# Last MLP: seven block products for the first matrix, the second matrix by pairs of hidden blocks over all tokens, and sums of weight blocks made by adding DMAs during the first MLP

## The chip, the cores and the metric

The kernel runs on one core of one Trainium2 chip. The metric is device time in microseconds (us) from the first to the last instruction of one launch; lower is better. Several executions are timed, and one more is recorded by the hardware profiler. All line numbers below are those of the profile: for the kernel before, "L231" is line 231 of the listing printed further down.

## The reference, cut to what matters

A trunk of two layers works on 1024 tokens with 1024 features. Layer 0 mixes tokens with an mLSTM, layer 1 with latent attention (MLA). After each mixer comes an MLP with a hidden width of 4096.

```python
def sqrelu_mlp(h, w1, w2):
    return jnp.square(jax.nn.relu(h @ w1)) @ w2

# in each layer
h = modulate(rmsnorm(x, g), shift, scale)
x = x + gate * rmsnorm(sqrelu_mlp(h, w1, w2), g2)
```

Everything is float32. `w1` is 1024 x 4096 and `w2` is 4096 x 1024 in each layer. The change concerns `h @ w1` and `... @ w2` of layer 1, for the second half of the tokens.

## The kernel before

**Numbers.** A float32 product is made of three products of a shorter format. Every operand is split into a high part (a cast on ScalarE, L189 for weights) and a low part (a subtraction on VectorE, L190), and `mm3` (L230 to L233) issues three matmuls for each pair of operand tiles: high weight and low weight against high and low data, without the product of the two low parts.

**Stages.** The tokens are worked on in two halves of 512, `hfs[0]` and `hfs[1]`. The four MLP calls run one after another, and the other work is woven between their steps: `mlp(0, hfs[0])` with the background `bg_latent` (the remaining adaLN vectors, the rope tables, the preparation of the latent weights), `mlp(0, hfs[1])` with the layer-1 mixer of the first half, `mlp(1, hfs[0])` with the layer-1 mixer of the second half, and last `mlp(1, hfs[1])`, called here the last MLP. Beside the last MLP runs only `all_out`, the writing of the results: `x_to_rows` transposes the residual stream into rows, `rows_out` normalises the MLP output, adds the residual and stores.

**One MLP.** The hidden width is cut into 32 blocks of 128. `hidden(f)` (L952) makes one block: 8 slices of the 1024 features times 3 matmuls, each 128 x 128 weights against 512 tokens, into one PSUM tile `ps`. ScalarE squares the ReLU of it (L962, L963) and casts it (L471), VectorE makes the low part (L472). `up_rows` (L978) multiplies four hidden blocks by the second matrix for two token blocks at a time, into a PSUM tile `pm` of two banks, and `accumulate` (L971) adds the result to the output in SBUF (VectorE, L198). Steps of both kinds alternate, 24 matmuls of 512 columns each. A step's weights (512 KB) are loaded two steps ahead (`AHEAD`, L944): SyncE's DMA into `raw` (4 buffers), L189 and L190 into `ws` (8 buffers, two per load).

**Order.** Each engine has one queue, in the order that a scheduler gives to the program's instructions. `paced()` (L182) ties an instruction of a background behind the latest weight split, L190. GpSimd has almost nothing to do in this kernel: small DMAs at the start and memsets that claim buffers (L170, L1346). `small(n)` (L144) hands out tiny tiles from 6 buffers.

Of the kernel before, what the change touches and what calls it, by code (L numbers as in the profile page):

```python
# [9 lines left out]
F32 = mybir.dt.float32  # L10
# [72 lines left out]
def kernel(  # L83
# [143 lines left out]

    pe_last = [None]

    def mm3(o, lh, ll, rh, rl, start, stop):  # L230
        nc.tensor.matmul(o, ll, rh, start=start, stop=False)  # L231
        nc.tensor.matmul(o, lh, rl, start=False, stop=False)  # L232
        pe_last[0] = nc.tensor.matmul(o, lh, rh, start=False, stop=stop)  # L233


    nc.scalar.preload_act_table_set("natural_log_exp_and_others")
# [240 lines left out]
    def normed(h, xs_, rstd, A, sh):  # L477

        for k in range(KD):
            with paced():  # L480
                nc.vector.scalar_tensor_tensor(
                    xs_[k], xs_[k], A[:, k : k + 1], rstd, ALU.mult, ALU.mult
                )
                split_mod(h.hi[k], h.lo[k], xs_[k], sh[:, k : k + 1])
            if k % 4 == 3:
                yield 1

# [455 lines left out]
    NF = DFF // P  # L943
    AHEAD = 2  # L944

    def mlp(l, hf, y, sizes, rows=False):


        w1, w2, h = mlp_w1[l], mlp_w2[l], hf.h2
        hids = {}  # L950

        def hidden(f):  # L952
            def hid(w):
# [98 lines left out]
        steps, prev, f0 = [], [], 0  # L1052
        for G in sizes:
            fs = list(range(f0, f0 + G))
            f0, done = f0 + G, 0
            for i in range(G):
# [7 lines left out]
        for n in range(len(steps) + AHEAD):  # L1064
            if n < len(steps):
                ready.append(steps[n][0]())
            if n >= AHEAD:
                yield from steps[n - AHEAD][1](ready.pop(0))

                yield steps[(n - AHEAD + 1) % len(steps)][1].__name__  # L1070


    rope_d = scratch([2, P, S], "rope_d")
# [494 lines left out]

    def x_to_rows(half):

        for k in range(KD):
            a, b = tmc(), tmc()
            nc.sync.dma_start(a, xs_blk(k, half))
            yield
            pt = pc()
            for t in range(4):
                nc.tensor.transpose(pt[:, ts(t, P)], a[:, ts(t, P)], ident)
            nc.scalar.copy(b, pt)
# [19 lines left out]
    def rows_out(hf, y, B):  # L1598

        xt = []  # L1600
        for t in range(4):
            a = k4v()
            r0 = hf.i * H + t * P
            nc.sync.dma_start(a, xr[r0 : r0 + P, :].rearrange("p (a b) -> p a b", b=512))
            xt.append(a)
        yield
        for t in range(4):
            yt, st = y.t[t], small(4)
            for g in range(2):
                junk = ps()  # L1610
                nc.scalar.activation(junk, yt[:, g], AF.Square, accum_out=st[:, g : g + 1])
            ys = [tmc(), tmc()]
            v, r, w = small(1), small(1), small(1)
            with tc.high_priority(PRIO):
                for g in range(2):
                    nc.vector.tensor_mul(ys[g], yt[:, g], B[:, g])
                nc.vector.tensor_scalar(v, st[:, 0:1], st[:, 1:2], 1.0 / D, ALU.add, ALU.mult)
                nc.vector.tensor_scalar_add(v, v, EPS)
                rsqrt_(r, v, w)
            for g in range(2):  # L1620
                nc.vector.scalar_tensor_tensor(ys[g], ys[g], r, xt[t][:, g], ALU.mult, ALU.add)
                r0 = hf.i * H + t * P
                nc.sync.dma_start(out[0, r0 : r0 + P, ts(g, 512)], ys[g])
            yield


# [126 lines left out]
    A1 = gain(2, NG(0, 2), adac(0, SC2))  # L1753
    B1 = gate(3, NG(0, 3), adac(0, G2))

    def post(hf, y, B, src, A, sh):
# [5 lines left out]
        yield 0  # L1762
        hf.h2 = Split()
        yield from normed(hf.h2, y, rstd, A, sh)

# [124 lines left out]
    drain(p1)  # L1890
    two_streams(f0, behind(bg_latent(), 4))
    rope_perm()


    z1 = FH(claim=True)
    ya = [None, None]

    def mixer1(hf, z, attention):
# [12 lines left out]
        for _ in wout(b_w_out[0], hf.o, lambda m, pt: evac(y[m], pt)):  # L1911
            yield 0
        yield 1
        yield from post(hf, y, B2, x_cols, A3, adac(1, SH2))
# [5 lines left out]
    two_streams(mlp(1, hfs[0], u0, [2] * 16, True), mixer1(hfs[1], z1, attention_second))  # L1920
    u1 = FH(claim=True)

    def all_out():
        yield from x_to_rows(0)
# [43 lines left out]
```

## Time and profile before

| what | value |
|---|---|
| median of three runs | 2379.76 us (2376.8 to 2380.19) |
| the profiled execution's own time | 2377.5 us |
| its span, first to last instruction | 2375.5 us |
| granted TensorE clock, mean | 0.997 |
| loads of MLP weights, first and last start | 463.1 us and 2326.6 us |

A row of busy time gives, for each engine (PE is TensorE's matmuls, PEld its weight loads, DVE is VectorE, ACT is ScalarE, POOL is GpSimd, SP is SyncE), microseconds and the number of instructions. A group's row gives line, engine, operation, output and input tiles, count, total busy time, mean duration in ns, then the idle time of its engine just before, with what ended it. A DMA row gives packets, megabytes and the share of 16 DMA engines' time.

### The profile page before, as it was taken

Reading aid. Unit: us, or ns where it says so; the run is one execution under the profiler, and the core shown is the slowest. Engines: PE = TensorE matmul, PEld = TensorE weight load, DVE = VectorE, ACT = ScalarE, POOL = GpSimd, SP = SyncE. Lnnn points to the kernel's source line nnn. Section 1 sums busy time; section 2 is a strip of 40 time slices with the busy share of each in tenths; the row PEclk is TensorE's granted clock in tenths of the full one; section 3 lists DMA queues with packets and bytes.
Section 4 is the critical chain, followed back from the end, with each engine's and each line's share of the span. In section 5 each row is a group of like instructions: output and inputs, shape, how many; then the busy total and the mean of one; then the engine's idle time right before and its main releaser. Section 6 shows DMA issues by size and latency. Waiting matters only on the chain.

```text
span 2375.5 us, 30534 instructions
## 1 busy us (share of the span) xinstructions
PE 2343.4 (99%) x11621; PEld 1946.7 (82%) x11621; DVE 1549.6 (65%) x2435; ACT 1055.6 (44%) x1716; POOL 18.2 (1%) x93
## 2 busy tenths in 40 slices
PE   7999999999999999999999999999999999999998
PEld 5888888788888888888888888888888888888887
DVE  6667866868666667877764967765666486353345
ACT  4355334655333454434443554444444453444333
POOL 1000000000000000000000000000000000000000
PEclk9999999999999999999999999999999999999999
DMA  9452664544664745555543454874434354364431
GB/s 313 149 142 85 186 181 139 168 133 144 186 181 143 250 135 187 160 161 183 182 133 113 147 166 163 249 248 136 148 98 143 114 169 129 102 191 140 144 102 62
DMA packets 377106, 374.48 MB, mean 158 GB/s; under 512 B 24355, under 2 KB 282464, under 8 KB 376960
## 3 DMA queue, kind: packets, MB, share of 16 engines
q1 hardware_dynamic: 376672, 372.44, 50.3%
q8 instruction: 91, 1.49, 0.3%
q14 instruction: 55, 0.45, 0.1%
q0 software_dynamic: 288, 0.10, 0.0%
HBM read 313.24 MB, written 59.24 MB: 157 GB/s over the span
## 4 chain that ended last, share of the span: by engine, by line
PE 89%; DVE 4%; DMA 4%; ACT 1%; issue 1%; SPq 0%; DVEq 0%; ACTq 0%
PE ps L231 16%; PE ps L233 16%; PE ps L232 16%; PE pm L231 9%; PE pm L232 9%; PE pm L233 9%; PE pc L1450 1%; DMA raw<-in_a_w_in_dram 1%; DMA raw<-in_mlp_w_dram 1%; PE pc L231 1%; PE pc L233 1%; PE pc L232 1%; PE pm L1336 1%; DVE wl L190 1%; PE pm L820 1%
## 5 line engine op out<-in xcount | busy, mean ns | idle before, releaser
L190 DVE TENSOR_TENSOR wl<-raw,wh 128x1024 fp32r<-128x1024 f32 (+2 forms) x366 | 438.9, 1202 | 442.7 <-ACT wh L189 435.7
L189 ACT CAST wh<-raw 128x1024 fp32r<-128x1024 f32 (+2 forms) x366 | 377.6, 1035 | 704.3 <-PE ps L231 381.7
L231 PE MATMUL ps<-k,wl 128*128 128x512 f32 x1528 | 605.2, 396 | 2.5 <-ACT k L679 1.4
L233 PE MATMUL ps<-k,wh 128*128 128x512 f32 x1528 | 596.1, 390 | 0.0
L232 PE MATMUL ps<-k,wh 128*128 128x512 f32 x1528 | 595.6, 390 | 0.0
L231 PEld LDWEIGHTS ps<-k,wl 128*128 128x128 f32 x1528 | 287.0, 188 | 65.1 <-issue 2.9
L233 PEld LDWEIGHTS ps<-k,wh 128*128 128x128 f32 x1528 | 286.8, 188 | 61.7 <-issue 0.5
L232 PEld LDWEIGHTS ps<-k,wh 128*128 128x128 f32 x1528 | 287.2, 188 | 58.8 <-issue 1.7
L198 DVE TENSOR_TENSOR k<-k,pm 128x512 f32<-128x512 f32 (+1 forms) x254 | 211.0, 860 | 104.1 <-PE pm L233 103.6
L231 PE MATMUL pm<-hd,wl 128*128 128x512 f32 x512 | 200.9, 392 | 0.5 <-ACT hd L471 0.5
L232 PE MATMUL pm<-hd,wh 128*128 128x512 f32 x512 | 199.3, 390 | 0.2 <-DVE hd L472 0.2
L233 PE MATMUL pm<-hd,wh 128*128 128x512 f32 x512 | 199.2, 389 | 0.0
L231 PE MATMUL pm<-wh,hd 128*128 128x512 f32 x488 | 192.2, 394 | 1.6 <-ACT raw L1342 1.3
L232 PE MATMUL pm<-wl,hd 128*128 128x512 f32 x488 | 190.9, 391 | 0.0
L233 PE MATMUL pm<-wh,hd 128*128 128x512 f32 x488 | 190.2, 390 | 0.0
L359 DVE SCALAR_TENSOR_TENSOR tma<-raw,cond,tma 128x512 f32<-128x512 f32 x168 | 125.6, 748 | 20.4 <-DMA raw<-in_kv_ada_w_dram 14.4
L472 DVE TENSOR_TENSOR hd<-tmp,hd 128x512 fp32r<-128x512 f32 x128 | 88.3, 690 | 54.7 <-ACT hd L471 54.4
L1342 ACT ACTIVATE raw<-pm,sm 128x128 f32<-128x128 f32 (+3 forms) x64 | 47.5, 742 | 150.1 <-DVE sm L1341 121.8
L231 PEld LDWEIGHTS pm<-hd,wl 128*128 128x128 f32 x512 | 96.2, 188 | 20.8 <-ACT hd L471 0.9
L232 PEld LDWEIGHTS pm<-hd,wh 128*128 128x128 f32 x512 | 96.1, 188 | 20.5 <-DVE hd L472 0.5
L233 PEld LDWEIGHTS pm<-hd,wh 128*128 128x128 f32 x512 | 96.1, 188 | 20.2
L231 PEld LDWEIGHTS pm<-wh,hd 128*128 128x128 f32 x488 | 91.6, 188 | 22.3 <-ACT raw L1342 3.5
(354 smaller groups left out, 3426.2 us busy)
## 6 DMA issues: line engine op xcount, KB each, us to landing
raw<-in_mlp_w_dram SPq DMA_DIRECT2D x256, 512.0 KB, 4.2
raw<-in_ada_w_dram SPq DMA_DIRECT2D x80, 512.0 KB, 4.2
raw<-in_a_w_in_dram SPq DMA_DIRECT2D x48, 512.0 KB, 4.8
xs<-k SPq DMA_DIRECT2D x40, 256.0 KB, 4.8
raw<-in_kv_ada_w_dram SPq DMA_DIRECT2D x16, 512.0 KB, 4.0
raw<-in_a_w_out_dram SPq DMA_DIRECT2D x16, 512.0 KB, 4.8
kd<-k SPq DMA_DIRECT2D x32, 256.0 KB, 3.8
vd<-k SPq DMA_DIRECT2D x32, 256.0 KB, 4.5
```

The lines of the kernel that those rows point to most:

```text
L189: nc.scalar.copy(hi[:, :n], r[:, :n])
L190: i = nc.vector.tensor_sub(lo[:, :n], r[:, :n], hi[:, :n].bitcast(F32))
L198: return f(*a, **k)
L231: nc.tensor.matmul(o, ll, rh, start=start, stop=False)
L232: nc.tensor.matmul(o, lh, rl, start=False, stop=False)
L233: pe_last[0] = nc.tensor.matmul(o, lh, rh, start=False, stop=stop)
L359: nc.vector.scalar_tensor_tensor(acc, r[:, kk], cond[:, k : k + 1], acc, ALU.mult, ALU.add)
L472: nc.vector.tensor_sub(lo, u, hi.bitcast(F32))
L820: nc.tensor.matmul(nv[:, r, i], hf.PT[p_][:, r, cs], v[2 * p_ + r], start=g == 0, stop=True,)
L1336: nc.tensor.matmul(o[:, :w], qh, kh, start=False, stop=True)
L1342: nc.scalar.activation(pr[:, :n], f, AF.Exp, bias=m, scale=SCALE, accum_out=l)
L1450: nc.tensor.transpose(pt[:, ts(2 * e + i, P)], u.prs[i][:, ts(b + e, P)], ident)
```

## The change

**The first matrix of the last MLP.** Two hidden blocks (256 hidden columns), 1024 features and 512 tokens are taken as a product of 2 x 2 blocks: features in two halves of 512, tokens in two halves of 256, hidden columns in two blocks of 128. The Strassen-Winograd form computes it with seven block products in place of eight, from sums of data blocks and sums of weight blocks. `pair` does this in four steps (`first`: products 1 and 2, `second`: 6 and 7, `third`: 5 and 4, `fourth`: 3). A product is 4 slices x 3 matmuls of 256 columns. The partial results are put together in PSUM by further accumulation, by three copies on ScalarE and by three additions on VectorE.

**The second matrix of the last MLP.** `up_by_f` takes two hidden blocks per step and all four token blocks, and holds two `pm` tiles over two steps; the matmuls, loads and accumulations are as many as before. Weights are asked for three steps ahead instead of two (`early`).

**The data blocks.** `quarters` replaces `normed` for the second half of layer 1: it keeps the normalised values and makes seven split tiles `B[1]` to `B[7]`; three of them are made later, at the 61st step of `mlp(1, hfs[0])`.

**The weight blocks.** `weight_sums` writes the four sums of each pair into a DRAM scratch `sums`, 16 pairs of 4 x 256 KB, with DMAs on GpSimd's queue, half of them adding to what stands in the scratch. In each of its 21 iterations VectorE sets a flag behind the pace, GpSimd copies it, and the DMAs of that iteration stand behind the copy. `with_weight_sums` advances it at every third yield of the first MLP.

**The output.** `x_to_rows` loads one block ahead, `rows_out` loads its rows as it goes, uses another buffer for the squares' unused output, and `all_out` advances at every second step.

The diff, cut to its core:

```diff
-    def mm3(o, lh, ll, rh, rl, start, stop):
+    def mm3(o, lh, ll, rh, rl, start, stop, more=False):
...
+    def weight_sums(w):
+        n = NF // 2
+        a = lambda p_, f, kh: wcols(w, (2 * p_ + f) * P, P, 4 * kh, 4)
+        o = lambda p_, i: by_k(sums[p_][:, ts(i, H)])
+        for m in range(n + 5):
+            flag, seen = small(1), small(1)
+            with paced():
+                nc.vector.memset(flag, 0.0)
+            now = nc.gpsimd.tensor_copy(seen, flag)
+            with tc.issue_after(now.ins):
+                put = nc.gpsimd.dma_start
+                add = lambda o_, i_: put(o_, i_, accum_op=ALU.add)
+                if m < n:
+                    put(o(m, 1), a(m, 1, 0))
+                    put(o(m, 2), a(m, 1, 0))
+                if 0 <= m - 1 < n:
+                    add(o(m - 1, 1), a(m - 1, 0, 0))
+                    add(o(m - 1, 2), a(m - 1, 1, 1))
+                if 0 <= m - 2 < n:
+                    put(o(m - 2, 0), o(m - 2, 1))
+                if 0 <= m - 3 < n:
+                    add(o(m - 3, 0), a(m - 3, 1, 1))
+                if 0 <= m - 4 < n:
+                    put(o(m - 4, 3), o(m - 4, 0))
+                if 0 <= m - 5 < n:
+                    add(o(m - 5, 3), a(m - 5, 0, 1))
+            yield
...
+        def pair(p_):
+            N = 256
+            cut = lambda t: t[:, :N]
+            u = Half()
+            def product(i, o, w, start=False):
+                (wh, wl), (bh, bl) = w, B[i]
+                for k in range(4):
+                    mm3(o, wh[:, k], wl[:, k], bh[k], bl[k], start and k == 0, k == 3, more=not start)
...
+            def first(w):
+                u.b, u.x, u.s, u.r = cut(ps()), cut(pc()), tmp(), tmp()
+                product(1, u.b, w[0], True)
+                with tc.high_priority(PRIO):
+                    u.s1 = cut(tmc())
+                    nc.scalar.copy(u.s1, u.b)
+                product(2, u.x, w[1], True)
+                with tc.high_priority(PRIO):
+                    c = cut(u.s)
+                    nc.vector.tensor_add(c, u.s1, u.x)
+                    nc.scalar.activation(c, c, AF.Relu)
...
+            return [
+                (lambda: pieces(wload([(0, 0, wcols(w1, 2 * p_ * P))], P)), first),
+                (from_sums(0), second),
+                (with_a22, third),
+                (one_tile, fourth),
+            ]
+        def up_by_f(fs, i, last):
...
+                for t in range(4):
...
+                        mm3(
+                            o, hh[:, ts(t, P)], hl[:, ts(t, P)], w[0][:, q], w[1][:, q],
+                            not e and q == 0, e == 1 and q == 1,
+                        )
+                    if e:
+                        accumulate((t, g), y.t[t][:, g], o)
...
+            for i in range(0, G if B else 0, 2):
+                p1, p2, p3, p4 = pair(fs[i] // 2)
+                ups = [up_by_f(prev, i + e, False) for e in range(2) if prev]
+                final = fs[i] + 2 == NF
+                steps += [p1] + late + ups[:1] + [p2]
+                steps += [p3, p4] + ups[1:] if final else ups[1:] + [p3]
+                late = [p4]
...
+        early = AHEAD + bool(B)
...
+    def with_weight_sums(g):
+        bg = weight_sums(mlp_w1[1])
+        for n, v in enumerate(g):
+            if n % 3 == 1:
+                next(bg, None)
+            yield v
+        drain(bg)
...
-    two_streams(f0, behind(bg_latent(), 4))
+    two_streams(with_weight_sums(f0), behind(bg_latent(), 4))
...
+    def quarters(y, rstd):
...
+        yield from normed_kept(y, rstd, A3, adac(1, SH2))
+        part(1, 0, 0)
+        part(2, 1, 0)
...
-    u1 = FH(claim=True)
+    u1 = FH()
...
-    dense = mlp(1, hfs[1], u1, [4] * 8, True)
+    dense = mlp(1, hfs[1], u1, [4] * 8, True, B)
+    n = 0
     while (d := go(dense)) is not end:
-        if v != "last" and d != "within":
+        n += d != "within"
+        if v != "last" and d != "within" and n % 2:
```

Three places show how instructions move. The first is TensorE in the last MLP. Before, at the end of a hidden block: `ps` is that block's PSUM tile, `k4` are tiles of the split data, `wh` and `wl` the split weights, `pm` the tile of the second matrix, `hd` a hidden block.

```order
L231 MATMUL ps_3401_19422<-k4_2970_16833,wl_3386_19342 128x512
L232 MATMUL ps_3401_19422<-k4_2971_16834,wh_3385_19341 128x512
L233 MATMUL ps_3401_19422<-k4_2970_16833,wh_3385_19341 128x512
L231 MATMUL pm_3403_19452<-wh_3391_19378,hd_3360_19141 128x512
L232 MATMUL pm_3403_19452<-wl_3392_19379,hd_3360_19141 128x512
L233 MATMUL pm_3403_19452<-wh_3391_19378,hd_3360_19141 128x512
```

In the changed kernel, in the last MLP's first pair, at the border of products 5 and 4 (`ps` and `pc` are the PSUM tiles `u.b` and `u.z`, `k4` tiles of split data sums, L232 to L234 are the lines of `mm3`):

```order
L232 MATMUL ps_3116_17682<-k4_3066_17423,wl_3115_17679 128x256
L233 MATMUL ps_3116_17682<-k4_3067_17424,wh_3114_17678 128x256
L234 MATMUL ps_3116_17682<-k4_3066_17423,wh_3114_17678 128x256
L232 MATMUL pc_3127_17742<-k4_3068_17429,wl_3115_17679 128x256
L233 MATMUL pc_3127_17742<-k4_3069_17430,wh_3114_17678 128x256
L234 MATMUL pc_3127_17742<-k4_3068_17429,wh_3114_17678 128x256
```

Each matmul of the first matrix takes 256 columns instead of 512, and a group into one PSUM tile has 12 matmuls in place of 24; the group behind it goes into another tile with the same pair of weight tiles.

The second place is GpSimd's queue. Before, the memsets that claim output tiles (`k4`) follow directly on one another:

```order
L170 MEMSET k4_770_4616 128x1 [waits PE_49]
L170 MEMSET k4_771_4617 128x1 [waits PE_49]
L170 MEMSET k4_772_4618 128x1 [waits DMAHW2_49,PE_49]
L170 MEMSET k4_773_4619 128x1 [waits DVE_49]
L170 MEMSET k4_1204_7294 128x1 [waits DVE_49,Pool_49]
L170 MEMSET k4_1205_7295 128x1 [waits DVE_49,Pool_49]
L170 MEMSET k4_1206_7296 128x1 [waits DVE_49,Pool_49]
```

After, one iteration of `weight_sums` in the steady state, with what each row waits for (`sm` are tiny tiles, `DMASW` counts the DMAs of this queue in eight semaphores, in turn):

```order
L976 COPY sm_1007_5961<-sm_1006_5960 128x1 [waits DVE_49]
L981 DMA sums_134<-in_mlp_w1_dram 128x4x128 [waits DMASW1_49]
L982 DMA sums_134<-in_mlp_w1_dram 128x4x128 [waits DMASW2_49]
L979 DMA sums_134<-in_mlp_w1_dram 128x4x128 [waits DMASW3_49]
L979 DMA sums_134<-in_mlp_w1_dram 128x4x128 [waits DMASW4_49]
L987 DMA sums_134<-sums_134 128x512 [waits DMASW5_49]
L979 DMA sums_134<-in_mlp_w1_dram 128x4x128 [waits DMASW6_49]
L991 DMA sums_134<-sums_134 128x512 [waits DMASW7_49]
L979 DMA sums_134<-in_mlp_w1_dram 128x4x128 [waits DMASW0_49]
L976 COPY sm_1020_6046<-sm_1019_6045 128x1 [waits DVE_49]
```

Eight DMAs per iteration now stand in this queue, each waiting for the one eight before it, and the next iteration's copy stands behind them all.

The third place is VectorE in the first MLP. Before (L359 and L341 belong to the adaLN vectors, `wl` are weight splits):

```order
L472 TENSOR_TENSOR hd_1014_6011<-tmp_1016_6037,hd_1014_6011 128x512 [waits Activation_49]
L190 TENSOR_TENSOR wl_1024_6081<-raw_1022_6078,wh_1023_6080 128x1024 [waits DMAHW1_49,PE_49,Activation_49]
L198 TENSOR_TENSOR k4_772_4618<-k4_772_4618,pm_1020_6048 128x1024 [waits PE_49]
L359 SCALAR_TENSOR_TENSOR tma_1007_5992<-raw_1021_6074,cond_71,tma_1007_5992 128x512 [waits DMAHW0_49,DVE_49]
L190 TENSOR_TENSOR wl_1030_6118<-raw_1028_6115,wh_1029_6117 128x1024 [waits DMAHW2_49,Activation_49]
L359 SCALAR_TENSOR_TENSOR tma_1007_5992<-raw_1021_6074,cond_71,tma_1007_5992 128x512 [waits DVE_49]
L190 TENSOR_TENSOR wl_1039_6179<-raw_1037_6176,wh_1038_6178 128x1024 [waits DMAHW3_49,PE_49,Activation_49]
L472 TENSOR_TENSOR hd_1025_6084<-tmp_1027_6110,hd_1025_6084 128x512 [waits Activation_49]
L198 TENSOR_TENSOR k4_773_4619<-k4_773_4619,pm_1031_6121 128x1024 [waits PE_49]
L341 TENSOR_REDUCE sm_1033_6152<-pc_1032_6147 128x4 [waits PE_49]
```

After, around two iterations (`sm` is the flag):

```order
L360 SCALAR_TENSOR_TENSOR tma_1027_6097<-raw_1030_6106,cond_71,tma_1027_6097 128x512 [waits DMAHW5_49,DVE_49]
L360 SCALAR_TENSOR_TENSOR tma_1027_6097<-raw_1030_6106,cond_71,tma_1027_6097 128x512 [waits DVE_49]
L190 TENSOR_TENSOR wl_1033_6113<-raw_1031_6110,wh_1032_6112 128x1024 [waits DMAHW6_49,Activation_49]
L975 MEMSET sm_1037_6147 128x1 [waits Pool_49]
L473 TENSOR_TENSOR hd_1034_6116<-tmp_1036_6142,hd_1034_6116 128x512 [waits Activation_49]
L198 TENSOR_TENSOR k4_772_4619<-k4_772_4619,pm_1042_6165 128x1024 [waits PE_49]
L190 TENSOR_TENSOR wl_1041_6162<-raw_1039_6159,wh_1040_6161 128x1024 [waits DMAHW7_49,Activation_49]
L360 SCALAR_TENSOR_TENSOR tma_1027_6097<-raw_1043_6191,cond_71,tma_1027_6097 128x512 [waits DMAHW0_49,DVE_49]
L360 SCALAR_TENSOR_TENSOR tma_1027_6097<-raw_1043_6191,cond_71,tma_1027_6097 128x512 [waits DVE_49]
L190 TENSOR_TENSOR wl_1046_6198<-raw_1044_6195,wh_1045_6197 128x1024 [waits DMAHW1_49,Activation_49]
L975 MEMSET sm_1050_6232 128x1 [waits Pool_49]
```

A memset that waits for GpSimd now stands behind every second weight split; the following splits, low parts (L473) and accumulations (L198) stand behind it in VectorE's queue.

More of the change, by code (lines that the diff above doesn't have):

```diff
@@ L1063, in mlp @@
         ready = []
-        for n in range(len(steps) + AHEAD):
+        early = AHEAD + bool(B)
+        for n in range(len(steps) + early):
             if n < len(steps):
                 ready.append(steps[n][0]())
-            if n >= AHEAD:
-                yield from steps[n - AHEAD][1](ready.pop(0))
-                yield steps[(n - AHEAD + 1) % len(steps)][1].__name__
+            if n >= early:
+                yield from steps[n - early][1](ready.pop(0))
+                yield steps[(n - early + 1) % len(steps)][1].__name__
     rope_d = scratch([2, P, S], "rope_d")
@@ L1762, in post @@
         yield 0
+        if kept:
+            yield from kept(y, rstd)
+            return
         hf.h2 = Split()
@@ L1913, in mixer1, with with_rest @@
         yield 1
-        yield from post(hf, y, B2, x_cols, A3, adac(1, SH2))
+        yield from post(hf, y, B2, x_cols, A3, adac(1, SH2), quarters if hf.i else None)
     two_streams(mlp(0, hfs[1], z1, [2] * 14 + [4]), mixer1(hfs[0], z0, attention_first), bg_rest())
     u0 = FH(claim=True)
-    two_streams(mlp(1, hfs[0], u0, [2] * 16, True), mixer1(hfs[1], z1, attention_second))
-    u1 = FH(claim=True)
+    def with_rest(g):
+        n = 0
+        for v in g:
+            if v != "within":
+                n += 1
+                if n == 61:
+                    later[0]()
+            yield v
+    two_streams(
+        with_rest(mlp(1, hfs[0], u0, [2] * 16, True)), mixer1(hfs[1], z1, attention_second)
+    )
+    u1 = FH()
     def all_out():
```

152 lines of the change are left out of this document (137 added, 15 removed).

## The prediction

> **What bounds the kernel now.** I read first the page's busy shares and the chain of work that ended last.
>
> ```profile
> span 2375.5 us, 30534 instructions
> PE 2343.4 (99%) x11621; PEld 1946.7 (82%) x11621; DVE 1549.6 (65%) x2435; ACT 1055.6 (44%) x1716; POOL 18.2 (1%) x93
> PE 89%; DVE 4%; DMA 4%; ACT 1%; issue 1%; SPq 0%; DVEq 0%; ACTq 0%
> ```
>
> TensorE is busy 99% of the span and holds 89% of the chain. A shorter kernel needs fewer or shorter matmuls, and a longer one any stall that reaches TensorE. The changed stage is the last MLP, so next comes the busy time by windows, for a stretch inside it (us, then busy time and count of PE, PEld, DVE, ACT, POOL, then granted clock, DMA share, GB/s).
>
> ```profile
> 2030.00:2370.00 340.00, 336.95 (x1504) 277.62 (x1503) 149.97 (x218) 135.15 (x213) 0.00 (x0) 1.00 0.40 124
> ```
>
> There TensorE is full at full clock; DVE (44%) and ACT (40%) have room. Here an instruction removed from TensorE is time removed. Busy means overlap, so the price of a matmul is the distance between starts, from the timeline. Between these two rows lies one hidden block of 24 matmuls (the first row is its first, the second is the first one behind it):
>
> ```profile
> 2301.51 0.39 PE L231 MATMUL ps<-k,wl 128*128 128x512 f32 x1
> ...
> 2306.95 0.39 PE L231 MATMUL pm<-wh,hd 128*128 128x512 f32 x1
> ```
>
> (2306.95 - 2301.51) / 24 = 226.7 ns for 512 columns. The last MLP has no 256-column matmuls, but an earlier projection has. Its timeline and its group of weight loads:
>
> ```profile
> 300.29 0.28 PE L231 MATMUL ps<-wh,k 128*128 128x256 f32 x1
> ...
> 302.44 0.28 PE L231 MATMUL ps<-wh,k 128*128 128x256 f32 x1
> ```
>
> ```profile
> L231 PEld LDWEIGHTS ps<-wh,k 128*128 128x128 f32 x49 | 9.3, 191 | 0.2
> ```
>
> From the first to the last of these L231 rows are six groups of three matmuls: 2.15 us / 18 = 119.4 ns for 256 columns. The weight load beside each lasts 191 ns, yet the spacing is below that: loads overlap each other here and do not set the pace.
>
> **The first matrix.** The groups of the last MLP:
>
> ```profile
> L231 PE MATMUL ps<-k,wl 128*128 128x512 f32 x256 | 101.1, 395 | 0.0
> L190 DVE TENSOR_TENSOR wl<-raw,wh 128x1024 fp32r<-128x1024 f32 x63 | 77.1, 1223 | 151.4 <-ACT wh L189 151.2
> L189 ACT CAST wh<-raw 128x1024 fp32r<-128x1024 f32 x63 | 66.4, 1053 | 177.1 <-PE ps L231 142.8 <-PE pm L232 34.3
> L198 DVE TENSOR_TENSOR k<-k,pm 128x512 f32<-128x512 f32 x59 | 38.0, 683 | 32.2 <-PE pm L233 32.2
> L472 DVE TENSOR_TENSOR hd<-tmp,hd 128x512 fp32r<-128x512 f32 x32 | 22.1, 692 | 17.5 <-ACT hd L471 17.5
> L962 ACT ACTIVATE tmp<-ps 128x512 f32<-128x512 f32 x32 | 18.9, 590 | 0.0
> ```
>
> Each of the three lines of `mm3` has 256 matmuls into `ps`: 768 x 226.7 ns = 174.1 us go. Added are 16 pairs x 7 products x 12 = 1344 matmuls of 256 columns: 1344 x 119.4 ns = 160.5 us. **Net -13.6 us.** The second matrix keeps its matmuls, loads and accumulations: 0.
>
> The Trainium skill ("TensorE: Matmul & The Clock Gate", section "Back-to-back issue gap") gives N/2.4 + 2.5 ns for an isolated matmul: 215.8 and 109.2 ns, and a sum of -19.0 us. The same section gives sustained figures of 81 ns for 128 and 131 ns for 512 columns; an estimate on the line between them is 98 ns for 256, which would make the change cost 1344 x 98 - 768 x 131 = +31 us. The trace disagrees with both, most with the second: 226.7 and 119.4 ns, a ratio of 0.53 where that line has 0.75.
>
> **What lies beside it.** Loads per pair of hidden blocks rise from 2 tiles to 3.5, so 16 x 1.5 = 24 more splits: 24 x 1.22 = 29 us of VectorE and 24 x 1.05 = 25 us of ScalarE. Three additions and three copies of 256 columns per pair are not in this stage; by the nearest row, the copy of 256 columns out of PSUM below, 48 x 0.37 = 18 us on each engine. In a stage of some 350 us that brings VectorE from 44% to about 58% and ScalarE from 40% to about 52%. They stay hidden: the casts' idle time (177.1 us) ends with TensorE freeing buffers (`ps`, `pm`), not with a DMA, so weights are early today.
>
> ```profile
> L671 ACT COPY k<-ps 128x256 f32<-128x256 f32 x3 | 1.1, 374 | 9.2 <-PE ps L233 9.2
> ```
>
> Whether a product must wait for an evacuation is not in the trace. The three PSUM tiles of a pair are written again after at least one other product (12 x 119.4 = 1.43 us), and a copy takes 0.37 us, an accumulation 0.68 us. Bounds are 0 and one lost accumulation-and-copy per pair, 16 x 1.05 = 17 us. I take the lower end, nearest to the copy's row, and **+1.5 us** once for the stage's start (the last data pieces, 0.69 us each by the row of L472, and two products without an `up` step between them) and keep 17 us for the range. The end is the same: behind the last matmul the output's chain runs to the end of the span, 8.9 us.
>
> ```profile
> 2366.57 0.39 PE L233 MATMUL pc<-wh,hd 128*128 128x512 f32 x1
> ```
>
> `quarters` adds 14 ACT copies and 14 + 8 DVE operations of about 0.69 us to `mlp(1, hfs[0])` and drops 8 subtractions there: some 10 us per engine, spread over steps in which the next window shows both with a third of the time free. Cost 0; uncovered it would be those 10 us. The removed memsets, the shifted loads of `x_to_rows` and the new buffer for the squares lie on engines that do not set the end: 0.
>
> ```profile
> 1950.00:2000.00 50.00, 50.00 (x228) 41.33 (x227) 35.66 (x50) 23.92 (x35) 0.39 (x4) 1.00 0.42 121
> ```
>
> **The weight sums.** Paced behind VectorE's splits, the 21 iterations fall into about 562 to 800 us, one every 10.9 us (two steps of 24 x 226.7 ns). The windows there, and what the casts and loads of that stretch show:
>
> ```profile
> 562.00:620.00 58.00, 58.00 (x261) 47.99 (x260) 48.01 (x70) 28.61 (x36) 0.10 (x1) 1.00 0.60 186
> 620.00:700.00 80.00, 79.04 (x356) 65.04 (x355) 49.60 (x64) 27.98 (x37) 0.00 (x0) 1.00 0.62 185
> 700.00:745.00 45.00, 45.00 (x200) 37.26 (x199) 19.51 (x24) 14.60 (x20) 0.00 (x0) 1.00 0.28 83
> 745.00:800.00 55.00, 55.00 (x245) 45.03 (x244) 46.23 (x76) 22.83 (x30) 0.00 (x0) 1.00 0.76 229
> L189 ACT CAST wh<-raw 128x1024 fp32r<-128x1024 f32 x47 | 48.5, 1050 | 93.1 <-DMA raw<-in_mlp_w_dram 67.5 <-PE ps L231 15.3 <-PE pm L231 10.3
> raw<-in_mlp_w_dram SPq DMA_DIRECT2D x41, 512.0 KB, 4.8
> ```
>
> The 16 DMA engines are taken for 0.60 x 58 + 0.62 x 80 + 0.28 x 45 + 0.76 x 55 = 138.8 of 238 us: 99 us are free. The price of a packet comes from two windows with one weight load each, in 512-byte pieces (498 to 504 us) and in 2-KB rows (843 to 847 us):
>
> ```profile
> DMA packets 1040, 0.52 MB, mean 87 GB/s; under 512 B 16, under 2 KB 1040, under 8 KB 1040
> q1 hardware_dynamic: 1040, 0.52, 30.2%
> DMA packets 272, 0.52 MB, mean 131 GB/s; under 512 B 16, under 2 KB 16, under 8 KB 272
> q1 hardware_dynamic: 272, 0.52, 37.2%
> ```
>
> 0.302 x 6 us x 16 / 1040 = 27.9 ns per 512-byte packet, and 0.372 x 4 x 16 / 272 = 87.5 ns per 2-KB packet. Per pair six transfers have 512 pieces (four of them add) and two have 128 rows: in all (96 x 512 x 27.9 + 32 x 128 x 87.5) / 16 = 108 us of all engines. No row shows an adding transfer or one from DRAM to DRAM. Lower bound is this copy price, since the same pieces move; upper bound is twice it for the 64 additions, which read two operands: 108 + 64 x 512 x 27.9 / 16 = 165 us. I take the copy price, being that of the rows nearest to it.
>
> The new wait is VectorE's memset. It needs a flag buffer that GpSimd's copy of three iterations before has read; that copy stands behind the DMAs of the iteration before it, each of which waits for the DMA eight earlier. So VectorE feels the DMAs only if they lag about five iterations, 54 us. Behind the memset stand the weight splits, low parts and accumulations, and TensorE waits for these. The last memset needs the transfers through iteration 15, by the same working 95 us at copy price: inside the 99 us, so it does not wait. The issue of a DMA on GpSimd is bounded by the rows of its start:
>
> ```profile
> 1.28 0.70 POOL L264 DMA_DIRECT2D raw<-in_norm_g_dram  x1 [0.34 <-issue]
> 5.10 0.50 POOL L264 DMA_DIRECT2D raw<-in_kv_latent_g_dram  x1
> ```
>
> These move 32 KB and 1 KB. At a fixed 0.50 to 0.70 us, 128 issues take 64 to 90 us, under 238 us and hidden. If the 0.20 us grew with the 31 KB, 256 KB would need 2.2 us, 282 us in all and 17 us per iteration against 10.9: then it is GpSimd that lags. I take the fixed price, as a 32-fold size changed it by less than half.
>
> Shared DMA engines make the first MLP's own loads slower. They now take 4.8 us, and 67.5 us of the casts' idle time end with them, so they arrive without much to spare. Bounds: 0, and a full second landing in each of the some five double steps of 745 to 800 us, where the DMA share is highest, 5 x 2 = 10 us. I take **+3 us**, near the lower end because TensorE stands full in these windows in spite of the share of 0.76.
>
> **Sum.** 2377.5 (the profiled execution's own time: 2375.5 of span and 2.0 around it) - 13.6 + 1.5 + 3 = 2368.4 us. The profiled execution lies below the median of the runs, 2379.76, and 1.4 us below their mean, (2380.19 + 2376.8 + 2379.76) / 3 = 2378.9; with these 1.4 us I predict **2370 us**.
>
> **Rivals.**
> *A wait in place of the matmuls (slower).* Adding transfers cost twice a copy. Place: VectorE's memset in 562 to 800 us. Through iteration 15, 54 of the 64 additions add 54 x 512 x 27.9 / 16 = 48 us to 95: 143 us against 99 free, and TensorE waits 44 us: 2377.5 - 13.6 + 1.5 + 44 + 1.4 = 2411 us. It decides from about 4 us over the free 99; up to the gain of 13.6 it only eats that. For it: nothing prices an addition, and the slack at copy price is only 4 us. Against it: five iterations of lag, and the transfers need only be done by the last MLP, 1200 us later. GpSimd's issue at 2.2 us would come out similarly (lag 6 us per iteration, 120 less 54 us).
> The Trainium skill ("Collectives: The Full Stack", section "The bandwidth ceiling: the fold count and why AG ≠ RS ≠ AR") says that an add in a DMA needs two source reads and so runs at half the rate. By that rule the sum is this rival's 2411 us; no run here shows an adding transfer.
> *Half the gain given back (no change).* Evacuation waits of 0.5 us in each pair (8 us), or the upper end of the load contention (10 us in place of 3), or both: 2375 to 2383 us. For it: a step of the first matrix becomes 2.9 or 1.4 us long where it was 5.4, and three casts follow close on one another; against it: the splits are early today.
> *Weight loads as the bound (much slower).* Were a 256-column matmul held to its load's 191 ns, 1344 x 191 = 257 us would replace 174.1: +83 us, about 2464. The spacing of 119.4 ns speaks against it.
> *Shorter spacing.* With the isolated spacing and no contention 2377.5 - 19.0 + 1.5 + 1.4 = 2361 us; the rows speak against it.
>
> **How the numbers follow.** Forecast 0.44, with its own range 2363 to 2375; the wait 0.29 (2385 to 2425); half given back 0.20; weight loads 0.02; shorter spacing 0.05. The range 2360 to 2412 leaves out the weight loads, the longer half of the wait's range (0.14) and little else. 0.2% is 4.8 us, about what a measurement of this kernel can tell from no change. Faster by more, below 2375: 0.44 + 0.05 = 0.49; within it 0.20; slower 0.31.
>
> **What would show it.** Right: from the start of the last MLP to the last matmul about 12 us less, with 256-column matmuls 119 ns apart; VectorE under 65% there; no idle time of TensorE in 562 to 800 us beyond 3 us; the memsets waiting for nothing. Wrong: memsets that end an idle time of VectorE on GpSimd, and TensorE's gaps behind weight splits there (the wait); a DMA share of 1.0 in those windows with longer landings of weights (contention); gaps of TensorE that end with a copy or an addition of the new steps (evacuation); spacing near 190 ns (weight loads).

## The result, and the profile after

The changed kernel takes 2464.95 us (median of four runs, 2460.75 to 2470.3) against 2379.11 us (2376.8 to 2380.19): 1.0363 times as long, with a 95% interval of 1.0339 to 1.0387. It was forecast at 2370 us, with a range from 2360 to 2412. The page of the changed kernel, in the order of the rows shown of before (busy shares, the two large DMA queues, the chain that ended last):

```profile
span 2468.5 us, 32278 instructions
PE 2358.4 (96%) x12197; PEld 1973.5 (80%) x12197; DVE 1606.9 (65%) x2550; ACT 1101.4 (45%) x1826; POOL 149.1 (6%) x238
...
q1 hardware_dynamic: 375392, 385.02, 50.5%
q0 software_dynamic: 39200, 33.66, 7.8%
...
PE 76%; DMA 12%; DVE 7%; ACT 2%; issue 1%; SPq 1%; DVEq 0%; ACTq 0%
```

TensorE fell from 89% to 76% of the chain and DMA rose from 4% to 12%: the kernel now waits for transfers. To find where, I set the starts of the matching matmuls of hidden blocks in the two traces beside each other. The distance is 0.7 us until 590 us of the time before, 44.7 us from 702 to 746 us, 74.8 us by 845 us, stays between 74.6 and 75.6 us up to the last MLP (2022 us), and ends at 93 us. So there are **two losses: 75 us in the first MLP, and 18 us in the last MLP**, where 13.6 us were to be gained.

**The first MLP.** The same four windows as in the prediction, in the changed kernel (us, busy time and count of PE, PEld, DVE, ACT, POOL, then granted clock, DMA share, GB/s):

```profile
562.00:620.00 58.00, 51.55 (x231) 42.10 (x229) 37.61 (x60) 22.13 (x28) 18.16 (x22) 0.99 0.91 209
620.00:700.00 80.00, 62.09 (x240) 49.64 (x241) 37.87 (x53) 17.80 (x24) 39.16 (x44) 0.86 1.08 246
700.00:745.00 45.00, 37.54 (x152) 30.19 (x151) 21.37 (x28) 12.46 (x16) 23.36 (x27) 0.89 1.19 257
745.00:800.00 55.00, 55.00 (x244) 45.47 (x243) 30.29 (x48) 21.16 (x29) 29.00 (x36) 1.00 1.20 263
```

In 620 to 700 us TensorE did 240 instructions in place of 356, and the DMA share is over 1, where 0.62 stood before. (A share over 1 means that packets of both queues were open on one engine at once.) The waits of 562 to 880 us, in total, times and longest:

```profile
ACT wh L189 <- DMA raw<-in_mlp_w_dram: 161.0, 35, 15.1
DVE wl L190 <- ACT wh L189: 109.2, 34, 13.2
...
PE ps L232 <- DVE sm L975: 43.2, 8, 9.0
```

The last row names the flag's memset as what TensorE waited for, and this is a row to distrust: the memset stands right behind the weight split in VectorE's order. All that the trace has on the memset's line:

```profile
L975 DVE MEMSET sm<- x21: 59/59/59, 561.6 to 865.1; 128x1 f32 x21
its engine sat idle before it (us, times) until:
who waited for it (us, times):
  POOL sm L976: 104.2, 15
```

VectorE was never idle in front of it (nothing is listed under "until"), and GpSimd's copy waited for it 15 of 21 times: GpSimd was early. The chain runs the other way: the weights land late, the cast waits for them (161.0 us; before, 67.5 us in 562 to 800 us), the split for the cast, TensorE for the split. The transfers of that stretch (packets, MB, share of 16 engines; then KB each and median us to landing):

```profile
q0 software_dynamic: 38912, 33.56, 60.1%
q1 hardware_dynamic: 48054, 43.15, 47.3%
...
raw<-in_mlp_w_dram SPq DMA_DIRECT2D x44, 512.0 KB, 13.2
```

A weight load took 13.2 us where it took 4.8. Its single packets did not get longer: over the whole trace, 512-byte packets of this queue took 27 ns in the median in both kernels.

**The last MLP.** Two windows of the changed kernel; before, TensorE was busy 100.00 of 100.00 us in each:

```profile
2100.00:2200.00 100.00, 94.79 (x602) 84.20 (x602) 45.57 (x57) 51.73 (x85) 0.00 (x0) 1.00 0.55 163
2200.00:2300.00 100.00, 92.74 (x572) 81.03 (x571) 62.74 (x108) 52.24 (x99) 0.00 (x0) 1.00 0.59 180
```

The timeline of one second step of `up_by_f` shows the gaps (start, duration, engine and line, and in brackets the idle time before with what ended it):

```profile
2213.01 0.40 PE L232 MATMUL pm<-wh,hd 128*128 128x512 f32 x1
...
2214.59 0.69 DVE L198 TENSOR_TENSOR k<-k,pm 128x512 f32<-128x512 f32 x1 [0.28 <-PE pm L234]
...
2215.34 0.50 PE L232 MATMUL pm<-wh,hd 128*128 128x512 f32 x1 [0.78 <-DVE k L198]
...
2217.45 0.68 DVE L198 TENSOR_TENSOR k<-k,pm 128x512 f32<-128x512 f32 x1
...
2219.37 0.68 DVE L198 TENSOR_TENSOR k<-k,pm 128x512 f32<-128x512 f32 x1
...
2220.10 0.50 PE L232 MATMUL pm<-wh,hd 128*128 128x512 f32 x1 [1.75 <-DVE k L198]
```

Token block 0 goes into the first bank of a `pm` tile. Its addition to the output, 2214.59, starts as soon as it is done. Token block 1 goes into the second bank of the same tile, and its first matmul waits at 2215.34 for that addition to end. So does block 3 behind the addition of block 2, which came later still because other work stood ahead of it on VectorE. The wait is written in the program, per tile and not per bank; TensorE's order at such a step reads

```text
L232 MATMUL pm_3519_20113<-wh_3513_20085,hd_3500_20031 128x512
...
L232 MATMUL pm_3519_20113<-wh_3513_20085,hd_3515_20102 128x512 [waits DVE_49]
```

where the second row is the first of block 1 (a row of L233 and one of L234 stand between). The kernel before adds both banks only after both are written, so no matmul writes into a tile that is being read. Over the last MLP this makes 28 waits (two in each of 14 steps; four of them are for ScalarE's copy of a first result, L202):

```profile
PE pm L232 <- DVE k L198: 18.9, 24, 1.8
...
PE pm L232 <- ACT k L202: 2.5, 4, 0.8
```

These are idle times only, 21.4 us. A wait costs somewhat more: behind the one at 2215.34 the next matmul starts 0.34 us later, where 0.23 us is usual. What the waits cost in all is measured below.

### The profile page after: what moved, and what is told of

It is laid out like the page before. It is cut to its first block, busy times and chain, and to the rows that moved or that the text cites. A ratio compares the mean times of both kernels' runs of the same rounds, so it can differ in the third digit from the quotient of the medians.

```text
span 2468.5 us, 32278 instructions
## 1 busy us (share of the span) xinstructions
PE 2358.4 (96%) x12197; PEld 1973.5 (80%) x12197; DVE 1606.9 (65%) x2550; ACT 1101.4 (45%) x1826; POOL 149.1 (6%) x238
## 4 chain that ended last, share of the span: by engine, by line
PE 76%; DMA 12%; DVE 7%; ACT 2%; issue 1%; SPq 1%; DVEq 0%; ACTq 0%
PE ps L232 13%; PE ps L233 13%; PE ps L234 13%; DMA raw<-in_mlp_w_dram 8%; PE pm L232 8%; PE pm L233 8%; PE pm L234 8%; PE pc L232 2%; PE pc L234 2%; PE pc L233 2%; DVE wl L190 1%; PE pc L1631 1%; ACT wh L189 1%; DMA raw<-in_a_w_in_dram 1%; DVE k L198 1%
## 5 line engine op out<-in xcount | busy, mean ns | idle before, releaser
L190 DVE TENSOR_TENSOR wl<-raw,wh 128x1024 fp32r<-128x1024 f32 (+2 forms) x382 | 459.0, 1203 | 477.3 <-ACT wh L189 392.9
L189 ACT CAST wh<-raw 128x1024 fp32r<-128x1024 f32 (+2 forms) x382 | 394.5, 1035 | 758.3 <-PE ps L232 229.7
L232 PE MATMUL ps<-k,wl 128*128 128x512 f32 (+1 forms) x1464 | 566.1, 387 | 51.9 <-DVE sm L975 43.2
L233 PE MATMUL ps<-k,wh 128*128 128x512 f32 (+1 forms) x1464 | 556.7, 380 | 0.0
L234 PE MATMUL ps<-k,wh 128*128 128x512 f32 (+1 forms) x1464 | 556.4, 380 | 0.0
L232 PEld LDWEIGHTS ps<-k,wl 128*128 128x128 f32 x1464 | 279.8, 191 | 110.2 <-DVE sm L975 45.9
L234 PEld LDWEIGHTS ps<-k,wh 128*128 128x128 f32 x1464 | 279.3, 191 | 53.0 <-issue 0.5
L233 PEld LDWEIGHTS ps<-k,wh 128*128 128x128 f32 x1464 | 279.8, 191 | 51.5 <-issue 1.7
L198 DVE TENSOR_TENSOR k<-k,pm 128x512 f32<-128x512 f32 (+1 forms) x254 | 212.8, 858 | 96.2 <-PE pm L234 95.6
L232 PE MATMUL pm<-wh,hd 128*128 128x512 f32 x488 | 196.1, 402 | 23.0 <-DVE k L198 18.9
L232 PE MATMUL pm<-hd,wl 128*128 128x512 f32 x512 | 200.9, 392 | 0.5 <-ACT hd L472 0.5
L233 PE MATMUL pm<-hd,wh 128*128 128x512 f32 x512 | 199.3, 390 | 0.2 <-DVE hd L473 0.2
L234 PE MATMUL pm<-hd,wh 128*128 128x512 f32 x512 | 199.2, 389 | 0.0
L234 PE MATMUL pm<-wh,hd 128*128 128x512 f32 x488 | 191.2, 392 | 0.0
L233 PE MATMUL pm<-wl,hd 128*128 128x512 f32 x488 | 190.6, 391 | 0.0
L232 PEld LDWEIGHTS pm<-wh,hd 128*128 128x128 f32 x488 | 91.7, 188 | 53.8 <-DVE k L198 28.5
L232 PEld LDWEIGHTS pm<-hd,wl 128*128 128x128 f32 x512 | 96.1, 188 | 20.9 <-ACT hd L472 0.9
L233 PEld LDWEIGHTS pm<-hd,wh 128*128 128x128 f32 x512 | 96.2, 188 | 20.7 <-DVE hd L473 0.5
L234 PEld LDWEIGHTS pm<-hd,wh 128*128 128x128 f32 x512 | 96.1, 188 | 20.0
L473 DVE TENSOR_TENSOR hd<-tmp,hd 128x512 fp32r<-128x512 f32 x128 | 88.0, 688 | 34.4 <-ACT hd L472 33.8
## 6 DMA issues: line engine op xcount, KB each, us to landing
sums<-in_mlp_w_dram POOLq DMA_DIRECT2D x96, 256.0 KB, 13.2
```

The source lines that it names most:

```text
L189: nc.scalar.copy(hi[:, :n], r[:, :n])
L190: i = nc.vector.tensor_sub(lo[:, :n], r[:, :n], hi[:, :n].bitcast(F32))
L198: return f(*a, **k)
L232: nc.tensor.matmul(o, ll, rh, start=start, stop=False, **m)
L233: nc.tensor.matmul(o, lh, rl, start=False, stop=False, **m)
L473: nc.vector.tensor_sub(lo, u, hi.bitcast(F32))
```

## The experiments

**The sums alone.** The kernel before, with `weight_sums` and `with_weight_sums` added and nothing that reads the sums:

```diff
+    def weight_sums(w):
...
-    two_streams(f0, behind(bg_latent(), 4))
+    two_streams(with_weight_sums(f0), behind(bg_latent(), 4))
```

> The kernel before with nothing but the weight sums added (their flags, copies and 128 DMAs in the first MLP; nothing reads the sums). Theory: the first MLP alone loses the 74.8 us seen between the two traces there, because its weight loads share the 16 DMA engines with the sums: 2379 + 75 = 2454 us, weight loads landing in about 13 us in place of 4.8. Rival: the stretch comes from the order of the rest of the changed program and not from the transfers: near 2379 us. The predicted wait of VectorE's memset on GpSimd would show as idle time of VectorE that ends with GpSimd in front of the memsets; the theory expects none.

2442.51 us against 2379.47, ratio 1.0267 (1.0252 to 1.0282): +63 us, 61.8 us of them by the end of the first MLP, and weight loads land in 11.9 us. VectorE is again never idle ahead of a memset. The sums alone (flags, copies and transfers) make the loss; the order of the rest is not needed for it. It is 13 us smaller than in the changed kernel. The two programs differ in the order of instructions there, and what of that makes 13 us was not tried.

**The last MLP alone.** The changed kernel without sums; the loads of the last MLP read rows of the second matrix in their place:

```diff
-                    wload([(0, 0, by_k(sums[p_][:, 2 * i * H : 2 * (i + 1) * H]))], P)
+                    wload([(0, 0, by_k(mlp_w2[1][(2 * p_ + i) * P : (2 * p_ + i + 1) * P, :]))], P)
...
-    two_streams(with_weight_sums(f0), behind(bg_latent(), 4))
+    two_streams(f0, behind(bg_latent(), 4))
```

> The changed kernel without the weight sums; the last MLP reads rows of the second matrix in the place of the sums, in transfers of the same size and shape, so its first-matrix values are not the reference's. Theory: only the last MLP's loss is left, 18 us over the kernel before: 2397 us. Rival (the two parts are not independent, late sums also hold up the last MLP): clearly under 2397, down to 2368.

2398.66 us, ratio 1.0082 (1.0067 to 1.0097): +19 us, as expected of the last MLP alone.

**The same, with additions by tile.**

```diff
-                    if e:
-                        accumulate((t, g), y.t[t][:, g], o)
+                    if e and t % 2:
+                        for n in range(2):
+                            accumulate((t - 1 + n, g), y.t[t - 1 + n][:, g], b[t // 2][:, n])
```

> As the run without sums, and up_by_f adds a PSUM tile's two banks to the output after both are written, as the kernel before does, instead of each bank at once. Theory: the wait of the matmuls into the second bank for the addition of the first (28 times, about 0.8 to 1.8 us) goes, and with it some 31 us: 2379 - 13.6 + 1 = 2366 us. Rival (the copies and additions of the seven products, or their later weights, hold TensorE up): no change against the run without sums, 2397 us.

2367.08 us, ratio 0.9951 (0.9934 to 0.9967). The 31.6 us went with the waits, and the windows are full again:

```profile
2100.00:2200.00 100.00, 100.00 (x616) 89.57 (x615) 64.18 (x111) 53.06 (x101) 0.00 (x0) 1.00 0.62 198
2200.00:2300.00 100.00, 100.00 (x644) 91.32 (x643) 54.25 (x71) 50.97 (x82) 0.00 (x0) 1.00 0.59 182
```

So the seven products themselves gave what was worked out: 12.4 us less than before (interval 8 to 16) against a sum of 13.6 less 1.5. Their copies, additions and extra weight splits are hidden.

**Plain copies in place of the additions.**

```diff
-                add = lambda o_, i_: put(o_, i_, accum_op=ALU.add)
+                add = lambda o_, i_: put(o_, i_)
```

> The changed kernel with plain transfers in place of the 64 adding ones, same pieces and order, so the sums are not sums. Theory A (adding reads two operands and costs twice a copy): the transfers fall back to about 108 us of the engines and the first MLP's loss nearly goes, 2465 - 60 = 2405 us. Theory B (any transfer from DRAM to DRAM in these pieces has the price seen, some 79 ns a packet in place of 28): little change, 2440 to 2465 us.

2433.71 us, ratio 1.0231 (1.0216 to 1.0247): 31 us less than the changed kernel, between the two theories. Its transfers over 562 to 900 us:

```profile
q0 software_dynamic: 10240, 33.56, 33.7%
...
raw<-in_mlp_w_dram SPq DMA_DIRECT2D x54, 512.0 KB, 7.4
```

0.337 x 338 us = 114 us of all engines for 128 copies, close to the 108 us that the prediction worked out at copy price. That the two agree is luck: the price was worked out for 512 packets of 27.9 ns in most transfers, and here a transfer had 80 packets (10240 / 128) of 178 ns on average. In the changed kernel the same bytes took 0.601 x 318 = 191 us; with 57 us for its 64 plain ones, 134 us are left for the 64 adding ones, against 57 us as copies. That is 2.35 times as much. The changed kernel's own trace, where the packets can be told apart by their size, gives more: 142 us for the 512-byte packets, which are those of the adding transfers, and 47 us for the 4-KB packets of the plain ones, 3.0 times. **An adding transfer took 2.35 to 3.0 times the engine time of a copy**, and 528 packets in place of 80 ((38912 - 64 x 80) / 64). The flags and the order are the same in both runs, so it is the transfers that make the difference. Theory A named this price, too low, and its forecast that the loss then nearly goes did not hold: copies alone still cost 34.8 us in the first MLP, and all of it before 700 us of the time before, which is 735 us of this run:

```profile
562.00:620.00 58.00, 58.00 (x261) 48.06 (x260) 44.60 (x69) 24.71 (x31) 17.39 (x28) 1.00 0.79 239
620.00:700.00 80.00, 59.42 (x235) 47.43 (x234) 36.56 (x51) 19.19 (x25) 30.99 (x45) 0.87 0.88 260
700.00:745.00 45.00, 40.22 (x167) 32.72 (x166) 20.11 (x28) 14.63 (x19) 18.40 (x30) 0.92 1.04 287
745.00:800.00 55.00, 55.00 (x244) 45.39 (x244) 33.33 (x54) 19.49 (x28) 23.98 (x37) 1.00 1.02 313
```

The prediction's own rows had this. From 562 to 700 us 0.40 x 58 + 0.38 x 80 = 54 us of the engines were free, and 12.7 iterations at the pace of 10.9 us want 73 us there (6.8 us each, but the first five are smaller, 21 us together): 19 us short. After 700 us 46 us are free for the 35 us that are left, and nothing more is lost. The 19 us explain a little over half of the 34.8. A part of the rest is the slower clock behind each gap (0.87 in 620 to 700 us; see the last section); how much was not worked out.

**The changed kernel with additions by tile only**, the same three lines as above:

> The changed kernel, with the additions of a PSUM tile's two banks made after both are written and nothing else altered. Theory: the loss of the last MLP goes and that of the first stays: 2465 - 31 = 2434 us. Rival (the two losses overlap): above 2440 us.

2434.61 us, ratio 1.0231 (1.0216 to 1.0247): 30 us less. The two losses add up.

**The sums spread out.** The additions by tile stay; the 21 iterations are spread over three MLPs:

```diff
-            if n % 3 == 1:
-                next(bg, None)
+            yields[0] += 1
+            if yields[0] % 16 == 1:
+                next(bg_sums, None)
...
-two_streams(mlp(0, hfs[1], z1, [2] * 14 + [4]), mixer1(hfs[0], z0, attention_first), bg_rest())
+two_streams(with_weight_sums(mlp(0, hfs[1], z1, [2] * 14 + [4])), mixer1(hfs[0], z0, attention_first), bg_rest())
```

> As the run before it, and the 21 iterations of the weight sums are spread over the first, second and third MLP, one every 16 yields (some 44 us and more) in place of every third yield of the first. Theory (the loss is the DMA engines' shortage while they serve the loads too): an iteration of some 12 us of all 16 engines in 44 us takes 0.27 beside a share of 0.5 to 0.6, which fits: 2367 + 3 = 2370 us, faster than both kernels. Rival (the adding transfers cost the same wherever they stand, by holding up each load that they meet, or GpSimd's memsets for the attention now wait behind them): 2400 us and more.

> As the run before it, one iteration every 9 yields (some 25 us). Theory: 0.49 of the engines beside 0.61 from 590 to 700 us is over 1, by 0.1 x 110 = 11 us, and again somewhat in 745 to 840 us: 2367 + 11 to 20 = 2378 to 2387 us, between the two paces. Rival (a fixed price per transfer): the same as one every 16 yields.

2406.98 us (ratio 1.011, 1.0088 to 1.0133) at 16 yields and 2431.37 us (1.0221, 1.0204 to 1.0238) at 9. Both forecasts failed, and the run at 16 yields came out where its rival had it, at 2400 us and more. The pace matters, but at 16 the mean share is no longer the explanation: 40 us are lost over the run without sums with additions by tile (33 us in the profiled execution, which is the fastest of its four). About 10 us of it come from the first iteration, which met no pace to stand behind, so that its flag was set at 2.4 us and its transfers ran beside the kernel's own first loads. The rest comes in steps of 1 to 5 us, after bursts of eight transfers.

**Two transfers at a time.** Each pair of transfers gets its own flag, every 4 yields, and none ahead of the first pace (against the run at 16 yields):

```diff
-            if yields[0] % 16 == 1:
+            if yields[0] % 4 == 2:
...
+            for i in range(0, len(todo), 2):
+                flag, seen = small(1), small(1)
...
+                    for g, o_, i_ in todo[i : i + 2]:
+                        g(o_, i_)
+                yield
```

> The sums by DMA over three MLPs, with additions by tile, two transfers at a time every 4 yields in place of eight every 16, and none ahead of the first pace. Theory (a burst of eight transfers, 12 us of all engines, holds up the loads that meet it): most of the 40 us over 2367 goes, 2370 to 2385 us. Rival (GpSimd's queue: its memsets for the attention wait behind the copy that waits for VectorE's flag, now four times as often): 2400 us or more.

2383.12 us, ratio 1.0016 (1.0006 to 1.0025): 24 us better with the same transfers, some 10 of them from the first iteration, and about what the kernel before takes. Of the remaining 16 us (19 in the profiled execution) 9 arise from 640 to 702 us, in the first MLP, where GpSimd has no memsets for the attention, so that rival does not explain them. Whether the others are loads held up, or those memsets behind the flags, was not separated.

**The sums on the chip.** No sums in DRAM: per pair, both weight blocks are loaded once and an engine makes the four sums in SBUF.

```diff
+            def load2():
+                with tc.high_priority(PRIO):
+                    a, b = u.wa, block(1)
+                    c, u.w3 = raw(), tmc()
+                    add(c[:, H:], b[:, :H], a[:, :H])
+                    add(c[:, :H], c[:, H:], b[:, H:])
+                    add(u.w3, c[:, :H], a[:, H:])
+                    u.wb = b
+                return halves(c)
+            def load3():
+                with tc.high_priority(PRIO):
+                    add(u.wb[:, :H], u.wb[:, :H], u.wb[:, H:])
+                return halves(u.wb)
```

> The last MLP with seven block products and the additions by tile; no sums in DRAM and no DMAs of GpSimd: VectorE makes the four sums of weight blocks of each pair from the two loaded blocks, 4 x 0.69 us per pair, 44 us in all beside its 57% in that stage. Theory: the first MLP loses nothing and VectorE's 70% stays beside TensorE: 2367 to 2370 us, faster than before by 0.4 to 0.5%. Rival (VectorE's longer queue delays the additions out of PSUM and so TensorE): above 2375 us.

> The same, with the four sums of each pair on GpSimd, which has nothing else to do in that stage. Theory: as the run before, 2367 to 2370 us, if an addition of 512 columns there takes no more than some 3 us (16 x 4 x 3 = 192 us in a stage of 340). Rival (GpSimd is slow enough, or holds VectorE up at the memory, that the splits come late): above 2380 us.

With `add` on VectorE 2367.59 us, ratio 0.9957 (0.9945 to 0.997): **faster than both kernels**. On GpSimd 2370.52 us, ratio 0.9966 (0.9953 to 0.9978); the two intervals overlap. In VectorE's version the last MLP keeps TensorE nearly full while VectorE is busy 66% to 75%:

```profile
2100.00:2200.00 100.00, 98.98 (x610) 88.58 (x609) 75.01 (x129) 54.48 (x104) 0.00 (x0) 1.00 0.49 154
2200.00:2300.00 100.00, 100.00 (x641) 91.17 (x640) 66.23 (x90) 49.87 (x81) 0.00 (x0) 1.00 0.50 153
```

## Why the prediction was wrong

**The first matrix: right.** The 13.6 us were priced by the spacing of matmuls. In the changed last MLP, from the first of these rows to the second are 12 matmuls of 256 columns:

```profile
2195.71 0.28 PE L232 MATMUL ps<-k,wl 128*128 128x256 f32 x1
...
2197.14 0.28 PE L232 MATMUL pc<-k,wl 128*128 128x256 f32 x1
```

1.43 us / 12 = 119 ns, as in the projection it was taken from (119.4), and the run without sums and waits has the gain. The rivals by shorter spacing and by weight loads fall. That the rival by weight loads was priced at 2464 us, the measured time, is chance: the 191 ns that it needs were not there.

**The second matrix "keeps its matmuls, loads and accumulations: 0": wrong, by 31 us.** The count is right. What failed is that only counts were compared: with two `pm` tiles held over two steps and each bank added at once, the matmuls of the second bank got a wait that the kernel before does not have. The changed kernel's text shows it (the addition moved out of "after both banks"), and so does the order of TensorE's instructions with their waits. It took the whole gain and 18 us more.

**"I take +3 us" for the first MLP's own loads: wrong, this term was 75 us.** The step that failed is the comparison of the work, 95 us, with 99 us free over the whole of 562 to 800 us. The term's upper bound of 10 us looked at 745 to 800 us alone, where the share was highest; 44 of the 75 us were lost before 702 us, where the shares were 0.60 and 0.62. Free time after 700 us is of no use to a load that is late at 650 us. By windows the sums were 19 us short before 700 us even at copy price, and the run with plain copies lost 34.8 us. The adding price makes it worse: 191 / 16 = 12 us per iteration against a pace of 10.9 us, which leaves nothing for the loads.

**The rival of twice the price: near in its price, wrong in its mechanism.** I expected surplus transfers to lag behind by themselves, for five iterations, until VectorE's memset stood still. The memset never waited. The two queues share the engines, and the loads of the first queue were slowed at once, from 4.8 to 13.2 us, while their lead is two steps. A backlog on one queue is paid by the other long before its own gate closes. The Trainium skill ("Collectives: The Full Stack", section "The bandwidth ceiling: the fold count and why AG ≠ RS ≠ AR") puts the reducing step of a ring of cores, whose add needs two source reads, at half the rate of the copying step; the 2.35 to 3.0 times measured here for an add from DRAM to DRAM agree in direction and lie above it.

**GpSimd's issue: right that it is hidden, wrong in its size.** An adding transfer took 1538 ns by its group's mean, twice the rows of the start, and all 128 issues some 150 us where 64 to 90 were forecast, but GpSimd was the one that waited (POOL L976 behind VectorE, 104.2 us).

## What to carry to other kernels

Compare transfers with free DMA time window by window, never over a stretch with different shares: a background transfer delays the loads beside it at once. A share that fits is not enough either, as the run at 16 yields showed, and two transfers at a time did better than eight. When matmuls are regrouped, count not only operations but which of them write into a tile that another engine is still reading; a PSUM tile of two banks is one tile to the program's waits. A sum that costs a spare engine 0.7 us in SBUF should not be made by a transfer.

## What the runs showed of the hardware

- An adding transfer of 256 KB from DRAM to DRAM is cut into 528 packets, a plain one of the same bytes into 80, and costs 2.35 to 3.0 times the engine time. Its 512-byte packets took 64 ns in the median in the changed kernel and 65 ns in the runs at 16 and at 4 yields, so crowding does not explain the price.
- A gap of TensorE costs more than its length. In 620 to 700 us the granted clock fell to 0.86 from 1.00, and 240 instructions took 62.09 us, 259 ns each, where 356 took 79.04 us, 222 ns each, before: 9 us of that window are slower matmuls and not idle time. The timeline shows it behind the longest wait: from 656.06 to 659.05 the matmuls are 427 ns apart, from 660.36 on 227 ns. The Trainium skill ("TensorE: Matmul & The Clock Gate", section "What's actually happening") says that the clock halves after an idle window of some 3.4 us. The longest wait there was 9.0 us, which agrees; behind a wait of 3.43 us (at 672.55) the spacing also grew to 427 ns, behind the 1.75 us at 2220.10 in the last MLP it stayed at 0.23 us.

```profile
655.47 0.80 PE L232 MATMUL ps<-k,wl 128*128 128x512 f32 x1 [8.96 <-DVE sm L975]
656.06 0.63 PE L233 MATMUL ps<-k,wh 128*128 128x512 f32 x1
...
659.05 0.63 PE L234 MATMUL ps<-k,wh 128*128 128x512 f32 x1
```

- GpSimd's addition of 512 columns takes about twice VectorE's (1.35 to 1.61 us by its four groups, against 0.69 us), and VectorE pays for it: with the sums on GpSimd its weight split took 1327 ns, with the sums on VectorE 1223 ns. The first row is of the run on VectorE, the second of the run on GpSimd, the third one group of that engine's additions:

```profile
L190 DVE TENSOR_TENSOR wl<-raw,wh 128x1024 fp32r<-128x1024 f32 x69 | 84.4, 1223 | 42.8 <-issue 13.8 <-ACT tmp L1026 10.3 <-PE pm L233 6.7
L190 DVE TENSOR_TENSOR wl<-raw,wh 128x1024 fp32r<-128x1024 f32 x70 | 92.9, 1327 | 84.2 <-ACT wh L189 42.1 <-issue 11.6 <-PE pm L233 9.9
L1061 POOL TENSOR_TENSOR tmc<-raw,raw 128x512 f32<-128x512 f32 x13 | 21.0, 1613 | 17.0 <-DVE wb L491 7.0 <-DVE sm L430 6.9 <-ACT tmc L1781 3.1
```
